# Splitting the first half of a transposed token tile into hi and lo in two steps of 256 columns

## The chip, the cores and the metric

One core of one Trainium2 chip runs the whole program. The metric is the device time of one execution in microseconds (us), as a median over runs. The engines are TensorE (PE), VectorE (DVE), ScalarE (ACT), GpSimd (POOL) and SyncE (SP, which issues the DMAs).

## The reference

The input is 256 tokens of width 1024. The computation, cut to its outline:

```python
x = x + 0.5 * swiglu(rms_norm(x), ...)                  # ffn1, hidden width 2816
x = x + token_mixer(rms_norm(x), ...)                   # three attentions, gated, then w_out
x = x + 0.5 * swiglu(rms_norm(x), ...)                  # ffn2
x = layer_norm(x); memn = layer_norm(mem)               # 256 memory rows
for l in range(2):
    h = x @ w_in[l]
    mix = concat(mla_mixer(h...), nsa_mixer(h...)) @ w_out[l]
    x = layer_norm(ALPHA * x + mix)
    x = layer_norm(ALPHA * x + memory_cross_attn(x, memn, ...))
    x = layer_norm(ALPHA * x + conv_ffn(x, ...))        # w_up, causal conv of 3, gate, w_down
```

All of it is in float32.

## The kernel before

**Products in two parts.** TensorE's operands are fp32r tiles. To keep float32 accuracy every operand is held as two such tiles, a rounded part (hi) and the remainder (lo), and `product` (L299) issues three passes over the contraction chunks: hi·hi for all chunks, then one lo times hi, then the other. `split` (L306) makes the two parts: ACT copies the source to hi (L307), and DVE subtracts hi from the source (L308).

**Token tiles.** The 256 tokens are two tiles of 128, t = 0 and t = 1. Before a matmul that contracts over the width, a tile of 128 tokens by 1024 columns has to be turned. `to_xT` (L357) does that in two halves, j = 0 and 1. `transpose` (L350) turns four blocks of 128x128 on PE into one PSUM tile `tp` of 128x512 (L354, two such buffers), and `split` writes columns j·4 to j·4+3 of `xTh` and `xTl`. So column c of `xTh` (128x128) is what matmul c of the first pass contracts, and columns 0 to 3 come from the first half, 4 to 7 from the second. There are 26 calls of `to_xT`: 24 on the stream itself, two on the memory tiles (there the tiles' names are `mTh` and `mTl`).

**Hand-overs.** `hand_over` (L367) stands between two stages: it turns tile 0, issues a unit of other work if there is one (`fill`: matmuls on the memory), and leaves tile 1 for the middle of the next stage's first unit (`later`, `flush`). `units` (L376) runs the next stage's matmuls, a column group of weights at a time, tile 0 and then tile 1. Weights come by DMA in pieces of 1 MB into two raw buffers `wraw`, and are split in steps of 512 columns into `whi` and `wlo` (`piece`, L282, by the same `split`).

**Order.** Each engine runs its instructions in a fixed order that the framework's scheduler makes from the program. An engine waits at an instruction until what it needs is done, and everything behind it on that engine waits too. So a place where PE needs `xTh` is a chain: four transposes, the copy on ACT, the first matmuls; and DVE's subtraction is needed only by the third pass.

Other names below: `xn` is the normalised tile of an rms norm (Square with its sum on ACT at L329, the product on DVE at L333), `X` the residual stream, `om` the output of nsa_mla, `lat` the latent of mla (its product on DVE, L970, which frees its PSUM tile), `late` the branch that the mixer adds last.

Of the kernel before, what the change touches and what calls it, by code (L numbers as in the profile page):

```python
# [190 lines left out]
class Kern:  # L191
# [165 lines left out]
    def to_xT(self, t, src, dst=None):  # L357

        hi, lo = self.half(dst or self.xT, t)
        for j in range(2):  # L360
            p = self.transpose(src[:, j * 512:j * 512 + 512], 4)
            self.split(hi[:, j * 4:j * 4 + 4], lo[:, j * 4:j * 4 + 4], p)

    def half(self, xT, t):
        return [z[:, :, t * P:t * P + P] for z in xT]
# [1048 lines left out]
```

## Time and profile before

| | |
|---|---|
| median of 3 runs | 1581.88 us (1580.79 to 1583.82) |
| the profiled execution's own time | 1585.94 us |
| its span | 1584.2 us |
| busy: PE, DVE, ACT, POOL | 97%, 68%, 50%, 9% |
| granted TensorE clock, mean | 0.993 |
| chain that ended last, by engine | PE 78%, DVE 9%, issue 5%, DMA 3%, ACT 3%, POOL 2% |

The span is what the profiler recorded of one execution; 1.74 us of that execution's time lie around it. The row of the chain follows the work back from the last instruction and says on which engine the time went. Busy shares are averages over stages.

### The profile page before, as it was taken

Reading aid. Unit: us, or ns where it says so; the run is one execution under the profiler, and the core shown is the slowest. Engines: PE = TensorE matmul, PEld = TensorE weight load, DVE = VectorE, ACT = ScalarE, POOL = GpSimd, SP = SyncE. Lnnn points to the kernel's source line nnn. Section 1 sums busy time; section 2 is a strip of 40 time slices with the busy share of each in tenths; the row PEclk is TensorE's granted clock in tenths of the full one; section 3 lists DMA queues with packets and bytes.
Section 4 is the critical chain, followed back from the end, with each engine's and each line's share of the span. In section 5 each row is a group of like instructions: output and inputs, shape, how many; then the busy total and the mean of one; then the engine's idle time right before and its main releaser. Section 6 shows DMA issues by size and latency. Waiting matters only on the chain.

```text
span 1584.2 us, 23791 instructions
## 1 busy us (share of the span) xinstructions
PE 1541.3 (97%) x8996; PEld 1328.0 (84%) x8996; DVE 1071.3 (68%) x2338; ACT 795.8 (50%) x1752; POOL 150.2 (9%) x158
## 2 busy tenths in 40 slices
PE   8999998999999999999999999999999999999997
PEld 6888876788778788889978988999898879889896
DVE  6756568565698755674676667776774666877675
ACT  5545445355545544444554436655454634456552
POOL 0000001010010000010010002312100010022211
PEclk9999999999999999999999999999999999999999
DMA  7664543444436655543544635554452426355550
GB/s 254 245 221 174 193 142 106 177 150 161 156 127 225 253 203 182 182 155 114 165 150 167 219 124 182 210 211 160 162 208 97 147 75 231 136 200 200 205 194 27
DMA packets 45573, 272.80 MB, mean 172 GB/s; under 512 B 5321, under 2 KB 9201, under 8 KB 16530
## 3 DMA queue, kind: packets, MB, share of 16 engines
q1 hardware_dynamic: 45458, 271.28, 48.1%
q8 instruction: 71, 1.16, 0.3%
q14 instruction: 44, 0.36, 0.1%
HBM read 265.98 MB, written 5.27 MB: 171 GB/s over the span
## 4 chain that ended last, share of the span: by engine, by line
PE 78%; DVE 9%; issue 5%; DMA 3%; ACT 3%; POOL 2%; SPq 0%; DVEq 0%; POOLq 0%; ACTq 0%
PE mm L304 54%; PE acc L304 12%; PE tp L354 3%; DVE wlo L308 3%; PE tp L1051 2%; PE acc L1095 1%; POOL ua L1263 1%; PE tp L1235 1%; PE tp L1129 1%; ACT whi L307 1%; POOL pr L322 1%; DMA wraw<-w_dn 1%; PE acc L1058 1%; PE acc L1220 1%; DMA wraw<-w_up 0%
## 5 line engine op out<-in xcount | busy, mean ns | idle before, releaser
L308 DVE TENSOR_TENSOR wlo<-wraw,whi 128x512 fp32r<-128x512 f32 (+2 forms) x928 | 601.8, 696 | 236.0 <-ACT whi L307 229.3
L307 ACT ACTIVATE whi<-wraw 128x512 fp32r<-128x512 f32 (+2 forms) x928 | 515.5, 619 | 313.3 <-PE mm L304 128.4
L304 PE MATMUL mm<-whi,xTh 128*128 128x512 f32 (+3 forms) x896 | 253.2, 401 | 5.8 <-ACT xTh L307 4.2
L304 PE MATMUL mm<-wlo,xTh 128*128 128x512 f32 (+3 forms) x896 | 240.2, 389 | 0.0
L304 PE MATMUL mm<-whi,xTl 128*128 128x512 f32 (+3 forms) x896 | 239.1, 388 | 0.0
L304 PEld LDWEIGHTS mm<-whi,xTh 128*128 128x128 f32 x896 | 162.8, 190 | 41.9 <-ACT xTh L307 8.2
L304 PEld LDWEIGHTS mm<-wlo,xTh 128*128 128x128 f32 x896 | 167.9, 189 | 35.5 <-issue 1.4
L304 PEld LDWEIGHTS mm<-whi,xTl 128*128 128x128 f32 x896 | 167.7, 188 | 34.1
L322 POOL TENSOR_TENSOR pr<-pv,mhalf 128x1 f32<-128x1 f32 (+3 forms) x44 | 45.7, 1038 | 902.8 <-DVE pv L320 898.1
L304 PE MATMUL mm<-xTh,whi 128*128 128x256 f32 x896 | 127.1, 284 | 3.2 <-DVE ua L1257 1.9
L304 PE MATMUL mm<-xTl,whi 128*128 128x256 f32 x896 | 125.9, 283 | 0.0
L304 PE MATMUL mm<-xTh,wlo 128*128 128x256 f32 x896 | 125.8, 283 | 0.0
L304 PEld LDWEIGHTS mm<-xTh,whi 128*128 128x128 f32 x896 | 116.6, 191 | 5.9 <-ACT th L1261 1.8
L304 PEld LDWEIGHTS mm<-xTl,whi 128*128 128x128 f32 x896 | 115.6, 192 | 0.0
L304 PEld LDWEIGHTS mm<-xTh,wlo 128*128 128x128 f32 x896 | 115.6, 192 | 0.0
L304 PE MATMUL acc<-whi,hh 128*128 128x512 f32 x352 | 112.4, 399 | 2.9 <-ACT hh L1265 2.9
L304 PE MATMUL acc<-wlo,hh 128*128 128x512 f32 x352 | 110.8, 394 | 0.2 <-DVE wlo L308 0.2
L304 PE MATMUL acc<-whi,hl 128*128 128x512 f32 x352 | 109.7, 392 | 0.0
L304 PEld LDWEIGHTS acc<-wlo,hh 128*128 128x128 f32 x352 | 66.6, 189 | 15.1 <-DVE wlo L308 0.7
L304 PEld LDWEIGHTS acc<-whi,hl 128*128 128x128 f32 x352 | 66.5, 189 | 14.3
L304 PEld LDWEIGHTS acc<-whi,hh 128*128 128x128 f32 x352 | 63.4, 189 | 15.1 <-ACT hh L1265 4.0
L1263 POOL TENSOR_TENSOR ua<-ua,ug 128x256 f32<-128x256 f32 x44 | 48.8, 1110 | 251.6 <-DVE ug L1262 175.6
(282 smaller groups left out, 1713.3 us busy)
## 6 DMA issues: line engine op xcount, KB each, us to landing
wraw<-w_ffn_gu SPq DMA_DIRECT2D x42, 1024.0 KB, 4.8
wraw<-w_up SPq DMA_DIRECT2D x40, 1024.0 KB, 4.8
wraw<-w_ffn_dn SPq DMA_DIRECT2D x22, 1024.0 KB, 4.7
wraw<-w_dn SPq DMA_DIRECT2D x22, 1024.0 KB, 4.8
wraw<-w_in_gate SPq DMA_DIRECT2D x12, 1024.0 KB, 4.9
gain<-vec SPq DMA_DIRECT2D x18, 512.0 KB, 4.2
wraw<-w_xk SPq DMA_DIRECT2D x8, 1024.0 KB, 4.7
wraw<-w_fea SPq DMA_DIRECT2D x8, 1024.0 KB, 4.7
```

Source lines behind the costliest of these rows:

```text
L304: self.nc.tensor.matmul(out, L[x], R[y], start=first and i == j == 0, stop=last and i == 2 and j == n - 1)
L307: self.nc.scalar.activation(hi, src, AF.Copy)
L308: self.nc.vector.tensor_tensor(lo, src, hi, op=ALU.subtract)
L322: self.nc.gpsimd.tensor_tensor(r, v, self.mhalf[:, :n], op=ALU.pow)
L354: self.nc.tensor.transpose(p[:, c], src[:, c * P:(c + 1) * P], self.ident)
L1051: nc.tensor.matmul(o[:, h], pt[:, h * (n // P) + k], v(k, h), start=k == 0, stop=k == n // P - 1)
L1058: nc.tensor.matmul(ps[:, h], qT[g][:, h0 + h, t * P:t * P + P], kT[g][:, h0 + h, :n], start=True, stop=True)
L1095: nc.tensor.matmul(pss[i][:, h], nqT[sl, r0 + h, t * P:t * P + P], skT[b][sl, :n], start=True, stop=True)
L1129: nc.tensor.matmul(ps[:30], kc2[:, s, :, :, i], w1[:, i * P:i * P + P], start=i == 0, stop=i == 15)
L1220: nc.tensor.matmul(ps[:, h], qT[:, k, t * P:t * P + P], kT[:, k], start=c == 0, stop=c == 1)
L1235: nc.tensor.matmul(o[:, 2 * h + c], v[:, k, ((h0 + h) * 2 + c) * P:((h0 + h) * 2 + c) * P + P], pt[:, 2 * h + k], start=k == 0, stop=k == 1)
L1263: nc.gpsimd.tensor_tensor(ua, ua, ug, op=ALU.mult)
```

## The change

```diff
     def to_xT(self, t, src, dst=None):
         hi, lo = self.half(dst or self.xT, t)
         for j in range(2):
             p = self.transpose(src[:, j * 512:j * 512 + 512], 4)
-            self.split(hi[:, j * 4:j * 4 + 4], lo[:, j * 4:j * 4 + 4], p)
+            for a, b in (((0, 2), (2, 4)), ((0, 4),))[j]:
+                self.split(hi[:, j * 4 + a:j * 4 + b], lo[:, j * 4 + a:j * 4 + b], p[:, a:b])
```

In each of the 26 calls the first half (j = 0) is split with two copies and two subtractions of 128x256, columns 0 and 1 and then columns 2 and 3, where there were one copy and one subtraction of 128x512. The second half and all other splits stay as they are. The transposes are the same. Line numbers behind L362 go up by one. Because the scheduler orders each engine's instructions anew, more than these rows move.

ACT at the two hand-overs into ffn2 (tile 0, then tile 1). `xTh` are the copies of the split, `xn,ss` the Square of tile 1's norm, `whi` the weights' copies, `th` the gate's first step. Before:

```order
L307 ACTIVATE xTh<-tp 128x4x128 [waits PE_49]
L329 ACTIVATE xn,ss<-X_74 128x1024 [waits DVE_49]
L307 ACTIVATE xTh<-tp 128x4x128 [waits PE_49]
L307 ACTIVATE whi<-wraw 128x512 [waits DMAHW6_49,Activation_49]
L307 ACTIVATE whi<-wraw 128x512 x3
L445 ACTIVATE th<-mm 128x256 [waits PE_49,Pool_49]
L307 ACTIVATE xTh<-tp 128x4x128 [waits PE_49] x2
L307 ACTIVATE whi<-wraw 128x512 [waits DMAHW0_49]
L307 ACTIVATE whi<-wraw 128x512 x3
```


The same place with the change:

```order
L307 ACTIVATE xTh<-tp 128x2x128 [waits PE_49]
L307 ACTIVATE xTh<-tp 128x4x128 [waits PE_49]
L329 ACTIVATE xn,ss<-X_74 128x1024 [waits DVE_49]
L307 ACTIVATE xTh<-tp 128x2x128 [waits DVE_49]
L307 ACTIVATE whi<-wraw 128x512 [waits DMAHW6_49,Activation_49]
L307 ACTIVATE whi<-wraw 128x512 x3
L446 ACTIVATE th<-mm 128x256 [waits PE_49,Pool_49]
L307 ACTIVATE whi<-wraw 128x512 [waits DMAHW0_49]
L307 ACTIVATE xTh<-tp 128x2x128 [waits PE_49]
L307 ACTIVATE xTh<-tp 128x4x128 [waits PE_49]
L307 ACTIVATE whi<-wraw 128x512
L307 ACTIVATE xTh<-tp 128x2x128 [waits DVE_49]
```


In tile 0 the second copy of 128x256 stands behind the second half's copy and behind the Square, and it waits for DVE. In tile 1 the first weight copy, which waits for a DMA, now stands ahead of the three copies of the tile, and another one between them.

PE at the two hand-overs into the second layer's conv_ffn (from the transposes of tile 0, `X_73`, on; `X_74` is tile 1). Before:

```order
L354 MATMUL tp<-c_ident,X_73 128x128 [waits DVE_49]
L354 MATMUL tp<-c_ident,X_73 128x128 x3
L354 MATMUL tp<-c_ident,X_73 128x128 [waits DVE_49,PE_49]
L354 MATMUL tp<-c_ident,X_73 128x128 x3
L304 MATMUL mm<-whi,xTh 128x512 [waits Activation_49]
L304 MATMUL mm<-whi,xTh 128x512 x3
L304 MATMUL mm<-wlo,xTh 128x512 x4
L304 MATMUL mm<-whi,xTl 128x512 [waits DVE_49]
L304 MATMUL mm<-whi,xTl 128x512 x3
```


With the change:

```order
L354 MATMUL tp<-c_ident,X_73 128x128 [waits DVE_49]
L354 MATMUL tp<-c_ident,X_73 128x128 x3
L354 MATMUL tp<-c_ident,X_73 128x128 [waits DVE_49,PE_49]
L354 MATMUL tp<-c_ident,X_73 128x128 x3
L304 MATMUL mm<-whi,xTh 128x512 [waits Activation_49]
L304 MATMUL mm<-whi,xTh 128x512
L304 MATMUL mm<-whi,xTh 128x512 [waits Activation_49]
L304 MATMUL mm<-whi,xTh 128x512
L304 MATMUL mm<-wlo,xTh 128x512 x4
L304 MATMUL mm<-whi,xTl 128x512 [waits DVE_49]
L304 MATMUL mm<-whi,xTl 128x512
L354 MATMUL tp<-c_ident,X_74 128x128 [waits DVE_49,PE_49]
```


The first pass over tile 0 is cut in two: its third matmul has a wait of its own. The transposes of tile 1, which wait for DVE's norm of `X_74`, have come forward into the third pass of tile 0's first unit.

ACT at the same place, from the copy of the last weights ahead of it on. Before:

```order
L307 ACTIVATE whi<-wraw 128x512 [waits DMAHW7_49,DVE_49,PE_49]
L307 ACTIVATE xTh<-tp 128x4x128 [waits PE_49]
L307 ACTIVATE xTh<-tp 128x4x128 [waits DVE_49,PE_49]
L307 ACTIVATE whi<-wraw 128x512 x3
L1280 ACTIVATE ux<-mm 128x512 [waits DMAHW5_49,PE_49]
L307 ACTIVATE xTh<-tp 128x4x128 [waits PE_49]
L307 ACTIVATE xTh<-tp 128x4x128 [waits DVE_49,PE_49]
```


With the change:

```order
L307 ACTIVATE whi<-wraw 128x512 [waits DMAHW7_49,DVE_49,PE_49]
L307 ACTIVATE xTh<-tp 128x2x128 [waits PE_49]
L307 ACTIVATE whi<-wraw 128x512
L307 ACTIVATE xTh<-tp 128x4x128 [waits DVE_49,PE_49]
L307 ACTIVATE whi<-wraw 128x512 x2
L307 ACTIVATE xTh<-tp 128x2x128 [waits DVE_49]
L307 ACTIVATE xTh<-tp 128x2x128 [waits PE_49]
L307 ACTIVATE xTh<-tp 128x2x128 [waits DVE_49]
```


Between the two copies of 128x256 of tile 0 there are now the second half's copy and three weight copies, and the second of them waits for DVE.

## Rows read from the trace of the kernel before

**Rows 1.** The page: busy time of each engine, its share of the span, instructions.
```profile
PE 1541.3 (97%) x8996; PEld 1328.0 (84%) x8996; DVE 1071.3 (68%) x2338; ACT 795.8 (50%) x1752; POOL 150.2 (9%) x158
```

**Rows 2.** Waits of PE: line, releaser: us in total, times, longest.
```profile
PE mm L304 <- ACT xTh L307: 4.8, 14, 0.7
...
PE acc L304 <- ACT hh L1265: 2.9, 3, 1.6
```

**Rows 3.** Groups by form: count, busy, mean ns of one, idle before and releaser.
```profile
L307 ACT ACTIVATE xTh<-tp 128x512 fp32r<-128x512 f32 x58 | 32.5, 594 | 47.5 <-PE tp L354 34.7 <-PE tp L1235 12.7
...
L307 ACT ACTIVATE hh<-tp 128x256 fp32r<-128x256 f32 x44 | 16.7, 379 | 3.9 <-PE tp L354 3.8
...
L308 DVE TENSOR_TENSOR xTl<-tp,xTh 128x512 fp32r<-128x512 f32 x58 | 38.2, 679 | 14.5 <-ACT xTh L307 14.5
...
L308 DVE TENSOR_TENSOR hl<-tp,hh 128x256 fp32r<-128x256 f32 x44 | 18.5, 419 | 4.9 <-ACT hh L307 4.8
```

**Rows 4.** Timeline, om of layer 0, tile 0: start, duration, engine, work, count.
```profile
842.87 1.26 ACT L307 ACTIVATE xTh<-tp 128x512 fp32r<-128x512 f32 x2 [3.08 <-PE tp L354]
...
843.52 1.19 PE L304 MATMUL mm<-whi,xTh 128*128 128x512 f32 x4
...
844.55 1.08 PE L304 MATMUL mm<-wlo,xTh 128*128 128x512 f32 x4
```

**Rows 5.** Timeline, mixer, tile 0 (ACT and PE).
```profile
200.72 0.60 ACT L307 ACTIVATE xTh<-tp 128x512 fp32r<-128x512 f32 x1 [4.00 <-PE tp L354]
...
201.21 1.05 ACT L329 ACTIVATE xn<-X 128x1024 f32<-128x1024 f32 x1
...
201.37 1.20 PE L304 MATMUL mm<-whi,xTh 128*128 128x512 f32 x4 [0.25 <-ACT xTh L307]
```

**Rows 6.** Timeline, ffn2, tile 0 (ACT and PE).
```profile
487.85 0.60 ACT L307 ACTIVATE xTh<-tp 128x512 fp32r<-128x512 f32 x1 [0.92 <-PE tp L354]
...
488.56 1.06 ACT L329 ACTIVATE xn<-X 128x1024 f32<-128x1024 f32 x1
...
488.50 1.19 PE L304 MATMUL mm<-whi,xTh 128*128 128x512 f32 x4 [0.25 <-ACT xTh L307]
```

**Rows 7.** Timeline, ffn2, tile 1 (ACT and PE).
```profile
494.71 1.09 ACT L307 ACTIVATE xTh<-tp 128x512 fp32r<-128x512 f32 x2
...
496.73 2.19 ACT L307 ACTIVATE whi<-wraw 128x512 fp32r<-128x512 f32 x4 [0.93 <-DMA wraw<-w_ffn_dn]
...
495.36 1.19 PE L304 MATMUL mm<-whi,xTh 128*128 128x512 f32 x4 [0.25 <-ACT xTh L307]
```

**Rows 8.** Timeline, conv_ffn of layer 1, tile 0, then tile 1's norm.
```profile
1381.41 1.07 ACT L307 ACTIVATE xTh<-tp 128x512 fp32r<-128x512 f32 x2
...
1382.05 1.20 PE L304 MATMUL mm<-whi,xTh 128*128 128x512 f32 x4 [0.33 <-ACT xTh L307]
...
1382.85 0.67 DVE L308 TENSOR_TENSOR xTl<-tp,xTh 128x512 fp32r<-128x512 f32 x1
...
1385.49 1.41 DVE L347 SCALAR_TENSOR_TENSOR X<-X,pr,gain 128x512 f32<-128x512 f32 x2
```

**Rows 9.** Timeline, om of layer 1, tile 1 (PE and DVE).
```profile
1294.82 1.19 PE L304 MATMUL mm<-whi,xTh 128*128 128x512 f32 x4 [0.25 <-ACT xTh L307]
...
1295.07 1.27 DVE L308 TENSOR_TENSOR xTl<-tp,xTh 128x512 fp32r<-128x512 f32 x2
```

**Rows 10.** Timeline, nsa_mla of layer 0, tile 1 (PE and DVE).
```profile
692.42 1.21 PE L304 MATMUL mm<-whi,xTh 128*128 128x512 f32 x4 [0.45 <-ACT xTh L307]
...
692.80 0.62 DVE L970 TENSOR_SCALAR lat<-mm,pr 128x384 f32<-128x384 f32 x1 [0.73 <-POOL pr L322]
```

**Rows 11.** Timeline, memory_attend of layer 0, tile 1 (PE and DVE).
```profile
874.73 1.33 PE L304 MATMUL mm<-xTh,whi 128*128 128x256 f32 x9 [0.30 <-ACT xTh L307]
...
874.81 1.28 DVE L308 TENSOR_TENSOR xTl<-tp,xTh 128x512 fp32r<-128x512 f32 x2
```

**Rows 12.** Timeline, late branch of the mixer, tile 1 (PE).
```profile
470.76 1.20 PE L304 MATMUL mm<-whi,xTh 128*128 128x512 f32 x4 [0.68 <-ACT xTh L307]
```


## The prediction, made before the changed kernel ran

> **What bounds the kernel now.** First the page's busy times: PE works 97% of the span, DVE 68%, ACT 50% [rows 1]. So a change is worth what it adds to PE's idle time or takes from it, and DVE and ACT matter only where PE waits for them. Next the list of PE's waits: the copies that the change touches (`xTh`, L307) end 14 waits of 0.7 us at most and 4.8 us in all [rows 2], 0.34 us each on average. That is the most that a faster copy could give, and it already says that a large gain isn't there. Then the durations by form, and for each hand-over the timeline of PE, ACT and DVE, laid beside the new order of the three engines.
>
> **What is removed and added.** Nothing leaves; each call gets one instruction more on ACT and one on DVE. The trace has the whole copy, 594 ns, and the whole subtraction, 679 ns, and no 128x256 form of either. The nearest rows are the copy and the subtraction of `hh`, PSUM to SBUF, 128x256: 379 and 419 ns [rows 3]. I take them as they are. So a call costs 2 x 379 - 594 = 164 ns more on ACT and 2 x 419 - 679 = 159 ns more on DVE; times 26 that is 4.3 and 4.1 us on engines with 50% and 32% idle. Spread out it is hidden under PE's matmuls; it costs only inside the hand-overs, which follow.
>
> **The chain at a hand-over.** The first copy still waits for all four transposes (in the order it waits for PE once, behind the fourth), so it starts no sooner. It ends 594 - 379 = 215 ns sooner, and PE's first two matmuls with it. The third matmul needs the second copy. In every hand-over of the new order that copy waits for DVE, and what it waits for is the subtraction of the first piece. So in place of one copy of 594 ns stands copy, subtraction, copy: 379 + 419 + 379 = 1177 ns, with two or three hand-offs between engines of some 0.04 us (the copy ends at 200.72 + 0.60 = 201.32, PE starts at 201.37 [rows 5]) about 1.26 us behind the start. In the kernel before, the third matmul starts 0.52 us behind the first: four of the first pass take 844.55 - 843.52 = 1.03 us [rows 4]; in the mixer that is 201.37 + 0.52 - 200.72 = 1.17 us behind the copy's start. With DVE free and nothing else in ACT's way the third matmul would thus be late by only 0.1 us. Below, "late" is the third matmul's new start less its old one; the passes behind it move with it.
>
> Why the second copy should wait for a subtraction that reads other columns: in the trace the subtraction follows its copy and the two are in a chain through `xTh`, so no row shows whether ACT and DVE could read one `tp` tile together. The Trainium skill, page "PSUM — Partial Sum Buffer", section "PSUM bank collisions raise a hardware error", says that two engines may not access one PSUM bank in the same partitions at once, reads against reads included, and that the compiler adds a dependency between them. By that rule splitting a tile that fills one bank can't let the subtraction of one half run beside the copy of the other; the order agrees (the wait is there), and no run here shows the collision itself. If the bank were no obstacle, the second copy would start when ACT is free; by my sum below that would take some 1.1 us of the 6.2 away (0.35 us at each place where DVE, not ACT, is what holds it), since at the other places ACT's own order holds the copy.
>
> **Place by place** (26 calls; PE's lost time, estimates from the rows).
> - *om, tile 0, both layers.* On ACT stand first copy, second half's copy, second copy. The pair took 1.26 us from 842.87 [rows 4], to 844.13; another 0.38 makes 844.5, so the third matmul starts at 844.5, where it stood at 843.52 + 0.52 = 844.04. Late 0.4 each (some overlap of neighbouring copies taken off): 0.8.
> - *Mixer, tile 0.* The Square (1.05 us from 201.21 [rows 5]) now stands between the two copies. It starts 0.21 earlier, ends at 202.05, the second copy at 202.43, the third matmul 202.48 for 201.89: 0.6.
> - *ffn2, tile 0.* Here both the second half's copy and the Square (1.06 us [rows 6]) stand between: 487.85 + 0.38 + 0.59 + 1.06 + 0.38 = 490.26, for a third matmul at 488.50 + 0.52 = 489.02. Less 0.1 to 0.2 for overlap: 1.1.
> - *ffn2, tile 1.* A weight copy that waits for its DMA (data at 496.73 [rows 7]) now stands ahead of the tile's copies, which began at 494.71. If the data comes at the same time, the first copy starts half a microsecond behind it, near 497.2, and the first matmul at 497.65 for 495.36: 2.3, of which 1.1 is the delay that tile 0 has made already. So 1.2 is new. The DMA's issue waits for a subtraction on DVE that itself stands behind the split now, so it may be later still. Against it: ffn2 runs on at the pace of its weights, and PE stops there anyway for what DVE or a DMA brings; I take 0.7, with 0 and 2.4 as ends.
> - *conv_ffn of layer 1, tile 0.* Four copies stand between the two pieces. Two took 1.07 us from 1381.41 [rows 8], so 0.48 to 0.54 each: 1381.41 + 0.27 + 4 x 0.48 + 0.38 = 1383.98, for 1382.05 + 0.52 = 1382.57. Late 1.4. DVE isn't what holds it: its subtraction began at 1382.85 and now ends 0.42 later. *Tile 1* there: its transposes now come after eight more matmuls of tile 0 (1383.98 + 8 x 0.23 = about 1385.9), and wait for a normalised half that was ready at 1385.49 + 0.7 = 1386.2 and moves back a little. PE loses about 0.3 more than the wait it had. Together 1.7.
> - *om of layer 1, tile 1.* DVE is held until 1295.07 [rows 9], so 1295.07 + 0.42 + 0.38 + 0.08 = 1295.95 for 1294.82 + 0.52 = 1295.34: 0.6.
> - *nsa_mla, tile 1, both layers.* Between second and third matmul the order now has matmuls of the next unit, into a PSUM tile that `lat` frees at 692.80 + 0.62 = 693.42 [rows 10]. The first two matmuls start at 692.42 - 0.21 and end by 692.8, so PE stands 0.7, less the 0.21 won, and a restart (0.1): 0.55 each, 1.1.
> - *memory_attend, tile 1, both layers.* Two short matmuls stand between. DVE is held until 874.81 [rows 11]: second copy done at 874.81 + 0.42 + 0.38 + 0.08 = 875.69; the first four now end by 874.73 - 0.21 + 4 x 0.13 = 875.04. So 0.65 less 0.21, 0.45 each: 0.9.
> - *Gains.* In the late branch, tile 1, the first copy now comes ahead of a weight copy, and the wait of 0.68 [rows 12] goes almost wholly: -0.6. At the mixer's and the first om's tile 1, other matmuls hide the second copy: -0.2 each. At the start the orders differ much: -0.3, within half a microsecond either way.
> - *Nothing* at the nine other calls, where units on the memory or whole passes of other matmuls lie between the copies and their readers. Without that cover each would cost 0.4 as in om.
>
> Sum: 0.8 + 0.6 + 1.1 + 0.7 + 1.7 + 0.6 + 1.1 + 0.9 - 1.3 = 6.2 us. On the profiled execution's own 1585.94 us (span 1584.2) that is 1592.1. That execution lies 4.06 us above the median of 1581.88; the same difference on the median gives **1588.1 us**. About 0.2% (3.2 us) is what a measurement of this kernel can tell from no change.
>
> **Rivals.**
> - *The split does what it says.* At all 14 waits PE starts 0.215 us sooner and the third matmul is on time: -3.0, 1578.9 us. For it: the difference of 594 and 379 ns is sure, and the plain chain makes the third matmul only 0.1 late, less than what is won if other matmuls stand between. It decides if the second copy ends within 0.57 us of the first's end; with DVE's 0.42 and its own 0.38 it can't, so only where there is cover. Chance 0.12.
> - *The delays are given back.* PE stops later in the same stage for something that isn't delayed, and the lost time is taken from that stop. For it: `hh` alone ends three waits of 2.9 us, one of 1.6 [rows 2], in the conv_ffn and ffn stages, which the two dearest places (ffn2 and layer 1's conv_ffn, 3.5 together) feed. If these 3.5 go, 2.7 stay: 1584.6, no change that can be told. Against it: what ACT and DVE make there is delayed by the same amount, since PE feeds them. Chance 0.23.
> - *ffn2's DMA decides.* Issue and landing move by the whole delay of DVE: 2.4 for 0.7, and the new order of the following weights adds as much again: 1588.1 + 3.4 = 1591.5. Chance 0.15.
> - My forecast, 1585.5 to 1590.5: 0.50.
>
> Outside the counted places the scheduler has reordered weight splits in ffn1 and both conv_ffn stages; PE's waits there are few, and I price them at nothing, within 2 us either way. Range: 1579.5 to 1593.5. It leaves out most of the first rival's lower half, and the third's upper end with these 2 us. Chances: the first rival's 1578.9 lies just at the bound, so half of its 0.12 is faster and half no change; of the second, 0.18 is no change, 0.03 faster and 0.02 slower; my forecast and the third are slower but for 0.01. Together: faster 0.09, within 0.2% 0.25, slower 0.66.
>
> **What would show it.** Right: copies of 128x256 near 380 ns, 52 on the 26 calls (48 to `xTh`, four to `mTh`); PE's waits for `xTh` grown from 4.8 to about 9 us, most of them at the third matmul; the Square between the copies in the mixer; a copy of the tile in ffn2 that begins after the weight's DMA landed. Wrong: third matmuls that don't wait; the lost time of ffn2 gone by the time memory starts; a copy of 256 columns well above 400 ns, by which every place would cost more.

## The result, and the profile after

The changed kernel took 1599.54 us (median of 6 runs, 1594.66 to 1604.27), beside 1582.85 us of the kernel before (6 runs): a ratio of 1.010 with a 95% interval of 1.0077 to 1.0122, some 16 us slower. Timed again with the later experiments it was 1.0085 (1.0068 to 1.0102). The profiled execution took 1596.49 us, with a span of 1594.7 us: 10.5 us more than the one of before. The runs of one kernel, before and after, differ by several us, so a median says more than one trace; the trace says where.

The page of the kernel after, part 1, answers to [rows 1]; below it are lines of its list of PE's waits, which answer to [rows 2] (us in total, times, longest).

```profile
PE 1545.0 (97%) x8996; PEld 1328.4 (83%) x8996; DVE 1073.6 (67%) x2364; ACT 798.4 (50%) x1778; POOL 150.8 (9%) x158
```

```profile
PE mm L304 <- ACT xTh L307: 10.8, 12, 2.8
...
PE acc L304 <- ACT hh L1266: 3.0, 3, 1.6
...
PE mm L304 <- DVE lat L971: 1.0, 2, 0.5
```

PE's waits for the copies went from 4.8 to 10.8 us, and the longest from 0.7 to 2.8. ACT and DVE are as idle as before. The groups by form (count, busy, mean ns, idle before) answer to [rows 3]:

```profile
L307 ACT ACTIVATE xTh<-tp 128x512 fp32r<-128x512 f32 x34 | 20.1, 595 | 15.5 <-PE tp L1236 13.4 <-PE tp L354 1.5
L308 DVE TENSOR_TENSOR xTl<-tp,xTh 128x256 fp32r<-128x256 f32 x48 | 20.0, 417 | 12.9 <-ACT xTh L307 12.7
L307 ACT ACTIVATE xTh<-tp 128x256 fp32r<-128x256 f32 x48 | 18.2, 378 | 45.9 <-PE tp L354 42.6 <-DVE xTl L308 3.1
```

The durations of the new instructions were right: 378 and 417 ns, for 379 and 419 taken from the `hh` rows. Both traces have the same 8996 matmuls, so the start of one and the same group of transposes in the two timelines tells by how much PE is late there:

| transposes (start of the group) | before | after | late by |
|---|---|---|---|
| mixer, tile 0 | 200.08 | 202.00 | 1.9 |
| ffn2, tile 0 | 487.21 | 487.98 | 0.8 |
| ffn2, tile 1 | 494.08 | 496.42 | 2.3 |
| memory, in ffn2 | 529.47 | 535.92 | 6.4 |
| om, layer 0, tile 0 | 842.23 | 849.13 | 6.9 |
| om, layer 0, tile 1 | 849.11 | 856.49 | 7.4 |
| conv_ffn, layer 0, tile 0 | 935.89 | 943.59 | 7.7 |
| nsa_mla, layer 1, tile 1 | 1147.58 | 1153.86 | 6.3 |
| om, layer 1, tile 0 | 1286.65 | 1294.98 | 8.3 |
| conv_ffn, layer 1, tile 0 | 1380.68 | 1390.51 | 9.8 |
| the last matmul | 1574.92 | 1585.49 | 10.6 |

The lag also falls in places, because the trace of before lost time of its own there: the granted clock has a mean of 0.66 at 212 to 217 us and of 0.57 at 970 to 974 us, where the trace after has 1.00 in the same matmuls, and two stops of PE near 1494 and 1502 us have no counterpart after.

More than half is lost in ffn2, between 488 and 506 us. Its timeline after (start, us, engine, work; at the end in brackets the idle time before and what ended it) answers to [rows 6, 7]:

```profile
488.61 1.03 ACT L307 ACTIVATE xTh<-tp 128x256 fp32r<-128x256 f32 x2 [0.92 <-PE tp L354]
489.82 1.06 ACT L329 ACTIVATE xn<-X 128x1024 f32<-128x1024 f32 x1 [0.18 <-DVE X L890]
490.79 0.19 ACT L329 ACTIVATION_READ_ACCUMULATOR xn<-X 128x1 f32 x1
490.88 0.36 ACT L307 ACTIVATE xTh<-tp 128x256 fp32r<-128x256 f32 x1
...
489.70 1.01 DVE L308 TENSOR_TENSOR xTl<-tp,xTh 128x256 fp32r<-128x256 f32 x2
490.63 0.68 DVE L308 TENSOR_TENSOR wlo<-wraw,whi 128x512 fp32r<-128x512 f32 x1
...
499.28 0.63 ACT L307 ACTIVATE whi<-wraw 128x512 fp32r<-128x512 f32 x1 [2.21 <-DMA wraw<-w_ffn_dn]
499.82 0.85 ACT L307 ACTIVATE xTh<-tp 128x256 fp32r<-128x256 f32 x2
...
491.30 0.73 PE L304 MATMUL mm<-whi,xTh 128*128 128x512 f32 x2 [1.51 <-ACT xTh L307]
...
496.42 1.03 PE L354 MATMUL tp<-c_ident,xn 128*128 128x128 f32 x8
500.23 3.40 PE L304 MATMUL mm<-whi,xTh 128*128 128x512 f32 x8 [2.78 <-ACT xTh L307]
503.43 1.40 PE L304 MATMUL mm<-wlo,xTh 128*128 128x512 f32 x4
...
491.39 0.33 SPq L291 DMA_DIRECT2D wraw<-w_ffn_dn  x1
```

In the trace of before, the same subtraction of a weight piece and the same DMA's issue:

```profile
488.44 0.69 DVE L308 TENSOR_TENSOR wlo<-wraw,whi 128x512 fp32r<-128x512 f32 x1
...
489.15 0.39 SPq L291 DMA_DIRECT2D wraw<-w_ffn_dn  x1
```

Tile 0: the second copy runs at 490.88, behind the Square, and PE stops 1.51 us at its third matmul. Tile 1: its transposes end at 497.45, but ACT is waiting for the data of `w_ffn_dn`, whose DMA was issued at 491.39 and in the trace of before at 489.15. The issue follows the end of a subtraction (`wlo`) that frees the raw buffer, at 491.31 for 489.13; on DVE that subtraction now stands behind two of the tile's. The copies of the tile, with nothing else to wait for, start at 499.82; PE stops for 2.78 us. And then the next eight matmuls, all hi·hi, take 3.40 us, where four took 1.07 elsewhere. The windows after (length, busy time and count for each engine, granted TensorE clock, DMA share, GB/s) show why:

```profile
core 0: us, PE busy (x) PEld busy (x) DVE busy (x) ACT busy (x) POOL busy (x), PEclk, DMA share, GB/s
...
497.00:500.00 3.00, 0.46 (x5) 0.22 (x2) 0.95 (x4) 0.79 (x3) 0.00 (x0) 1.00 0.85 269
500.00:503.00 3.00, 2.77 (x7) 2.14 (x8) 2.62 (x6) 2.50 (x6) 0.99 (x1) 0.62 0.78 291
503.00:506.00 3.00, 3.00 (x12) 2.49 (x11) 3.00 (x6) 0.17 (x1) 0.00 (x0) 0.81 0.05 22
506.00:510.00 4.00, 4.00 (x20) 3.26 (x19) 2.45 (x6) 2.68 (x6) 0.00 (x0) 1.00 0.45 147
```

Before the stop the granted clock is 1.00, the level of 2.4 GHz; behind it the clock is for a while at 1.2 GHz (0.62 and 0.81 are means of a stretch with both levels). The stop itself cost 2.5 us (2.78 less the 0.25 of before [rows 7]) and the matmuls behind it some 1.6 more: twelve of them take 4.60 us (500.23 to 504.83), where in the trace of before twelve take 3.02 from 495.36 on.

Two more places, the same timeline view after. At nsa_mla of layer 1, tile 1, other weight copies stand ahead of the second copy, and they too wait for a DMA:

```profile
1157.65 1.15 ACT L307 ACTIVATE whi<-wraw 128x512 fp32r<-128x512 f32 x2 [2.00 <-DMA wraw<-w_tok]
1158.70 0.36 ACT L307 ACTIVATE xTh<-tp 128x256 fp32r<-128x256 f32 x1
...
1156.41 1.07 PE L304 MATMUL mm<-whi,xTh 128*128 128x440 f32 x4 [0.46 <-DVE lat L971]
1157.32 0.56 PE L304 MATMUL mm<-wlo,xTh 128*128 128x440 f32 x2
1159.12 0.74 PE L304 MATMUL mm<-whi,xTh 128*128 128x512 f32 x2 [1.24 <-ACT xTh L307]
```

PE stops twice, 0.46 for `lat` as foreseen and 1.24 for the second copy, which was not. At conv_ffn of layer 1 it is as foreseen, the second copy behind three weight copies, at 1393.55 for an estimate of 1383.6 and a lag of 9.8:

```profile
1392.51 1.14 ACT L307 ACTIVATE whi<-wraw 128x512 fp32r<-128x512 f32 x2
1393.55 0.38 ACT L307 ACTIVATE xTh<-tp 128x256 fp32r<-128x256 f32 x1
...
1393.98 0.73 PE L304 MATMUL mm<-whi,xTh 128*128 128x512 f32 x2 [1.58 <-ACT xTh L307]
1394.55 1.51 PE L304 MATMUL mm<-wlo,xTh 128*128 128x512 f32 x4
1395.86 1.05 PE L304 MATMUL mm<-whi,xTl 128*128 128x512 f32 x2
1396.71 1.05 PE L354 MATMUL tp<-c_ident,X 128*128 128x128 f32 x4
1398.24 0.57 PE L304 MATMUL mm<-whi,xTh 128*128 128x512 f32 x1 [0.47 <-ACT xTh L307]
```

### The profile page after: what moved, and what is told of

It is laid out like the page before. It is cut to its first block, busy times and chain, and to the rows that moved or that the text cites. A ratio compares the mean times of both kernels' runs of the same rounds, so it can differ in the third digit from the quotient of the medians.

```text
span 1594.7 us, 23845 instructions
## 1 busy us (share of the span) xinstructions
PE 1545.0 (97%) x8996; PEld 1328.4 (83%) x8996; DVE 1073.6 (67%) x2364; ACT 798.4 (50%) x1778; POOL 150.8 (9%) x158
## 4 chain that ended last, share of the span: by engine, by line
PE 72%; DVE 11%; DMA 6%; issue 6%; ACT 3%; POOL 2%; SPq 0%; DVEq 0%; POOLq 0%; ACTq 0%
PE mm L304 49%; PE acc L304 10%; DVE wlo L308 4%; PE tp L354 3%; PE tp L1052 2%; DMA wraw<-w_up 2%; ACT whi L307 1%; PE acc L1096 1%; POOL ua L1264 1%; PE tp L1236 1%; PE tp L1130 1%; DMA wraw<-w_xo 1%; DMA wraw<-w_ffn_gu 1%; POOL pr L322 1%; DMA wraw<-w_tok 1%
## 5 line engine op out<-in xcount | busy, mean ns | idle before, releaser
L304 PE MATMUL mm<-whi,xTh 128*128 128x512 f32 (+3 forms) x896 | 256.6, 404 | 14.0 <-ACT xTh L307 10.3
L322 POOL TENSOR_TENSOR pr<-pv,mhalf 128x1 f32<-128x1 f32 (+3 forms) x44 | 48.9, 1112 | 908.3 <-DVE pv L320 904.7
L304 PEld LDWEIGHTS acc<-whi,hh 128*128 128x128 f32 x352 | 63.3, 188 | 15.8 <-ACT hh L1266 4.1
```

The costliest lines, as they stand in the source:

```text
L304: self.nc.tensor.matmul(out, L[x], R[y], start=first and i == j == 0, stop=last and i == 2 and j == n - 1)
L322: self.nc.gpsimd.tensor_tensor(r, v, self.mhalf[:, :n], op=ALU.pow)
```

## The experiments

All ratios are to the kernel before, measured next to it on the same chip, with 95% intervals.

**1. Both copies ahead of both subtractions.**

```diff
-            for a, b in (((0, 2), (2, 4)), ((0, 4),))[j]:
-                self.split(hi[:, j * 4 + a:j * 4 + b], lo[:, j * 4 + a:j * 4 + b], p[:, a:b])
+            for a, b in (((0, 2), (2, 4)), ((0, 4),))[j]:
+                self.nc.scalar.activation(hi[:, j * 4 + a:j * 4 + b], p[:, a:b], AF.Copy)
+            for a, b in (((0, 2), (2, 4)), ((0, 4),))[j]:
+                self.nc.vector.tensor_tensor(lo[:, j * 4 + a:j * 4 + b], p[:, a:b], hi[:, j * 4 + a:j * 4 + b], op=ALU.subtract)
```

> As the change, but both copies of the first half stand ahead of both subtractions in the code, so no copy waits for a subtraction; ACT's order then has the two copies side by side at all 26 calls. Theory A (the loss comes from the second copy's wait for DVE's subtraction and from what the scheduler puts ahead of it): the loss of 10.6 us of span vanishes, and the first matmul of each exposed hand-over starts 0.2 us sooner, so 2 to 4 us under the kernel before; no wait of PE for xTh over 0.7 us. Rival B (two small instructions for one, 8.4 us of ACT and DVE work, cost the time by themselves): still 8 to 17 us above the kernel before. Rival C (any new order of the schedule costs as much): 5 us or more above it, with new waits at other places.

Measured: 0.9992 (0.998 to 1.0004), median 1582.65 for 1584.62 us; the profiled span is 1580.1 us. In its list of PE's waits the copies have nearly vanished:

```profile
PE mm L304 <- ACT xTh L363: 0.7, 3, 0.3
```

It has every instruction of the change, in the same sizes, and none of its loss. That refutes rival B (the instructions' own cost) and C (any new order). The gain of the trace is some 4 us, that of the medians 2, which the interval can't tell from none. Place by place its trace shows what the shorter first copy is worth: the same matmul, by count, comes 0.2 us sooner behind each exposed hand-over (nsa_mla, om and memory_attend, in both layers).

**2. Two PSUM tiles for the two pieces.**

```diff
-        for j in range(2):
-            p = self.transpose(src[:, j * 512:j * 512 + 512], 4)
-            ...
+        for a, b in ((0, 2), (2, 4), (4, 8)):
+            p = self.transpose(src[:, a * P:b * P], b - a)
+            self.split(hi[:, a:b], lo[:, a:b], p)
```

> As the change, but the two pieces of the first half are transposed into two PSUM tiles of their own (three tiles a call, two buffers), so the first copy waits for two transposes and not four, and the second copy for no subtraction; the subtractions stay between the copies in the code. Theory A: no loss, and up to 0.4 us sooner at an exposed hand-over, 3 to 6 us under the kernel before, less what the third tile costs by waiting for a free buffer (the second half's copy goes back behind the weight copies at several places): between -5 and +2 us. Rival B: 8 to 17 us above the kernel before. Rival C: 5 us or more above.

Measured: 1.0039 (1.0025 to 1.0052), median 1590.18 for 1584.62, 5.6 us more; outside what theory A gave. Its second copy waits for no subtraction, yet PE waits for the copies 17 times, and the transposes of the third tile twice for a subtraction that has to free their buffer:

```profile
PE mm L304 <- ACT xTh L307: 9.0, 17, 1.7
...
PE tp L354 <- DVE xTl L308: 1.1, 2, 0.9
```

So it leaves a third of the loss and doesn't tell what the shared bank alone costs: other waits took the place of the one removed. The longest, 1.69 us before a matmul at 1388.2 in layer 1's conv_ffn, is once more copies that stand behind a weight copy, which waited 1.61 us for the DMA of `w_up`; the others are not taken apart.

**3. The change at the two calls into ffn2 alone** (`self.calls` counts the calls of `to_xT`).

```diff
+            cut = j == 0 and self.calls in (6, 7)
+            for a, b in ((0, 2), (2, 4)) if cut else ((0, 4),):
+                self.split(...)
```

> The change at the two hand-overs into ffn2 alone, the other 24 calls as before. Theory A, with the trace of the change: tile 0 loses 1.6 us, and tile 1 some 4.1, since a weight copy that waits for its DMA stands ahead of the tile's copies on ACT as in the change; so 4.5 to 6 us of span above the kernel before, all of it between 487 and 503 us. Rival D (PE's clock or the whole machine is slower with the change, the places do not add up): under 1 us. Rival B: 2/26 of the loss, under 1.3 us.

Measured: 1.0034 (1.0017 to 1.0051), median 1588.66 for 1584.62. The two calls alone cost 4 to 5 us, nearly what theory A says and more than rivals B and D allow. In the execution that was profiled the data had come in time: ACT took the weight copy at 497.06 without a wait for the DMA, PE's stops in ffn2 were 1.01, 0.45 and 0.55 us, the granted clock stayed at 1.00, and the span was 1583.3 us, no more than before. So in that execution the place cost nothing, and with data in time there was no long stop. That the other executions' cost hangs on when the DMA lands is likely, but one trace doesn't show it; the 12 runs spread from 1583.17 to 1598.02 us, the two longest at a mean granted clock of 0.985 where the shortest had 0.994. The mean of the twelve clocks is 0.991, that of the 32 runs of before beside them 0.9935.

**4. Subtraction in two steps, copy whole.**

```diff
+            self.nc.scalar.activation(hi[:, j * 4:j * 4 + 4], p, AF.Copy)
+            for a, b in (((0, 2), (2, 4)), ((0, 4),))[j]:
+                self.nc.vector.tensor_tensor(..., op=ALU.subtract)
```

> The copy of the first half stays whole, only its subtraction is made in two steps of 256 columns: DVE's half of the change alone. Theory A: nothing that can be told, -1 to +1.5 us, since the third pass that reads the result comes 1.8 us behind the first. Rival B: about half the loss, 5 to 8 us. Rival C: 5 us or more either way.

Measured: 0.9986 (0.9974 to 0.9997), median 1583.03 for 1584.62 us, a little below what theory A gave. DVE's half of the change costs nothing.

**5 to 7. The change again, without both calls into ffn2, and without tile 1's.** The condition of experiment 3 is always true, `self.calls not in (6, 7)`, and `self.calls != 7`.

> The change itself once more, beside the next three. 9 to 17 us above the kernel before. Theory F (part of the loss is TensorE's clock, which falls after the long stop at ffn2's tile 1): the executions lie in two groups, those with a mean granted clock of 0.992 or more 9 to 12 us above the kernel before, those at 0.990 or less 17 to 21 us above. Rival (the clock is the chip's affair, not the kernel's): the clocks of the four kernels of this call are spread alike.

> The change at all calls but the two into ffn2; there no weight copy stands ahead of tile 1's copies any more. Theory A, with the steps read from the trace of the change: 10.6 less the 5.7 of ffn2, so 4 to 6 us of span above the kernel before. Theory F: no execution under a granted clock of 0.990, so the median is 4 to 7 us above too. Rival C (any new order costs as much): 9 us or more.

> The change at all calls but the one for tile 1 into ffn2, whose first half is copied whole; the new order still has the weight copy, which waits for a DMA, ahead of that whole copy. Theory G (what costs there is the weight copy ahead on ACT, not the piece chain): the wait of 1.5 to 3 us before tile 1's first matmul in ffn2 stays, 8 to 16 us above the kernel before as with the change. Rival H (the chain of copy, subtraction and copy in tile 1 costs it): the stop shrinks to under 0.7 us, and the span to 5 to 7 us above the kernel before.

Measured: 1.0085 (1.0068 to 1.0102), 1.0049 (1.0034 to 1.0064) and 1.0101 (1.0074 to 1.0128). Without ffn2's two calls 7.7 us remain of 14 to 17; undoing tile 1's alone saves nothing. The two groups that theory F gave for experiment 5 did not show: its four runs were 1594.77 to 1599.46 at clocks of 0.989 to 0.992, not in order. What F says of experiment 6's clocks did: its four runs all had 0.993 and lay within 1.3 us, while those of experiment 7 had 0.987 to 0.993; but 7.7 us is more than the 4 to 7 that A and F gave. Experiment 7's 16 us by the ratio, 17 by the medians, lie at the upper end of theory G.

The clocks of all runs together speak against F's rival. The four sets of runs in which tile 0 of ffn2 is split as the change does it (the change twice, experiments 3 and 7) have mean clocks of 0.990 to 0.991; every other kernel here, the one of before and experiments 6 and 12 too, has 0.993 to 0.995. So the change's split of that tile brings the clock down, in some executions more than in others.

The timeline of experiment 7 in ffn2 (here lines are one higher):

```profile
500.57 0.38 ACT L449 ACTIVATE th<-mm 128x256 f32<-128x256 f32 x1 [4.99 <-PE mm L305]
501.50 0.63 ACT L308 ACTIVATE whi<-wraw 128x512 fp32r<-128x512 f32 x1 [0.54 <-DMA wraw<-w_ffn_dn]
502.03 1.07 ACT L308 ACTIVATE xTh<-tp 128x512 fp32r<-128x512 f32 x2
...
493.56 0.73 PE L305 MATMUL mm<-whi,xTh 128*128 128x512 f32 x2 [1.51 <-ACT xTh L308]
494.13 1.75 PE L305 MATMUL mm<-wlo,xTh 128*128 128x512 f32 x4
495.68 1.91 PE L305 MATMUL mm<-whi,xTl 128*128 128x512 f32 x4
...
502.67 1.19 PE L305 MATMUL mm<-whi,xTh 128*128 128x512 f32 x4 [1.32 <-ACT xTh L308]
```

The tile's copy is whole (128x512), and it stands behind the weight copy all the same, and PE stops 1.32 us. In this execution the clock fell already behind tile 0's stop of 1.51: the eight matmuls from 494.13 on end at 497.59, 3.46 us for 2.00 in the trace after (491.86 to 493.86), where the same stop left the clock at 1.00.

**8. Copies in two steps, subtraction whole.**

```diff
+            for a, b in (((0, 2), (2, 4)), ((0, 4),))[j]:
+                self.nc.scalar.activation(hi[:, j * 4 + a:j * 4 + b], p[:, a:b], AF.Copy)
+            self.nc.vector.tensor_tensor(lo[:, j * 4:j * 4 + 4], p, hi[:, j * 4:j * 4 + 4], op=ALU.subtract)
```

> The copy of the first half is made in two steps, the subtraction stays whole behind both: ACT's half of the change alone. Theory A: like the kernel with both copies first, -4 to 0 us, since no copy waits for a subtraction and the copies stand side by side. Rival B (more instructions cost): half of the loss, 4 to 8 us above.

Measured: 0.9985 (0.997 to 0.9999), median 1580.60 for 1582.62 us, as theory A gave.

**9 to 11. The second half split in place of the first; copies of 128 and 384 columns; experiment 8 again.** In 9 the pairs are `(((0, 4),), ((0, 2), (2, 4)))[j]`, in 10 `(((0, 1), (1, 4)), ((0, 4),))[j]` in the code of experiment 8.

> The change mirrored: the first half's split stays whole, the second half (columns 4 to 7) is split in two steps. As many added instructions, the same chain of copy, subtraction and copy, and in ffn2 again a weight copy that waits for its DMA between the two copies of tile 1; but its columns 6 and 7 are needed only by the second group of twelve matmuls, some 3 us behind the first matmul. Theory A: the loss is mostly gone, -2 to +3 us. Rival B (the added instructions cost) or rival C (any new order costs): 8 us or more above.

> Copies only, but in steps of 128 and 384 columns (one matmul's operand, then three), both ahead of the whole subtraction. Theory A: the first copy is another 0.1 us shorter, and the second, 0.49 us by the slope of the copies, ends when the second matmul wants it; -4 to -1 us against the kernel before, within 2 us of the steps of 256. Rival: the third instruction's fixed cost eats it, 0 to +2 us.

> The copies in two steps of 256 with a whole subtraction behind both, once more, beside the other two: -4 to 0 us against the kernel before, as in the first look (0.9985).

Measured: 1.001 (0.9995 to 1.0024), 0.9992 (0.9978 to 1.0007) and 0.9981 (0.9967 to 0.9995). The mirrored change has the same chain, and the same weight copies between its copies, and costs nothing that can be told: its columns are wanted late enough. That finer steps bring more isn't shown. Experiment 8's version has the two lowest ratios of the twelve, the second time 1579.87 for 1584.37 us, but the intervals overlap those of experiments 1, 4 and 10, so it can't be told from them; and experiment 4, which leaves the copy whole, lies as low as its first.

**12. The change without tile 0's call into ffn2** (`self.calls != 6`).

> The counterpart of the kernel that undid tile 1: the change at all calls but the one for tile 0 into ffn2. Tile 1 keeps the chain of copy, subtraction and copy, but in this order the weight copy that waits for its DMA stands behind its three copies again. Theory G (what costs in ffn2 is that weight copy ahead on ACT, with the stop of tile 0): tile 1's first matmul waits 0.5 us at most, and the time is that of the kernel with both ffn2 calls undone, 6 to 9 us above the kernel before. Rival H (tile 1's chain costs it): 11 us or more above.

Measured: 1.0043 (1.0023 to 1.0064), 1591.98 for 1583.87 us: the same as with both calls undone. In ffn2:

```profile
498.16 1.03 ACT L308 ACTIVATE xTh<-tp 128x256 fp32r<-128x256 f32 x2
499.56 0.38 ACT L308 ACTIVATE xTh<-tp 128x256 fp32r<-128x256 f32 x1 [0.36 <-DVE xTl L309]
501.87 2.20 ACT L308 ACTIVATE whi<-wraw 128x512 fp32r<-128x512 f32 x4 [1.92 <-DMA wraw<-w_ffn_dn]
...
500.00 0.73 PE L305 MATMUL mm<-whi,xTh 128*128 128x512 f32 x2 [0.67 <-ACT xTh L308]
```

The chain of tile 1 is here, bare: the second copy waits for DVE (0.36), PE 0.67 us. The weight's data comes as late as ever, 501.87, and nobody on the path waits for it. So of ffn2's loss the chain in tile 1 is half a microsecond, and the rest is tile 0's stop with the order that its split brings: rival H falls, theory G stands.

## Why the prediction was wrong

The direction and the cause were right, the size was not: 1588.1 forecast, range to 1593.5, 1599.54 measured. By its steps:

- **Durations, chain, and what the second copy waits for**: right, 378 and 417 ns. With the copies first the whole loss goes (experiment 1), and DVE's half alone costs nothing (4).
- **Places with the bare chain**: about right. The lag in the table grows by 0.5 at om, layer 0, tile 0 (0.4 forecast), and by 1.5 at ffn2, tile 0 (1.1). Taken at the same matmul by count it grows by 0.6 at nsa_mla of layer 0 (0.55), 0.5 and 0.2 at memory_attend (0.45 each) and 1.15 at om of layer 1 (1.0), and it shrinks by 0.6 in the late branch (0.6).
- **ffn2, tile 1: the step that failed.** The text saw the weight copy ahead of the tile's copies and the later issue of its DMA, and took "0.7, with 0 and 2.4 as ends", because ffn2 would make up for it. Measured: 6.4 - 2.3 = 4.1 us in the trace, and nothing made up: the lag is still 6.9 at om. The issue moved by 2.2 us and the data came 2.6 us later (499.28 for 496.73 [rows 7]); the stop, 2.5 us longer than the one of before, was just above the upper end of the range, and the clock behind it, of which the text had nothing, added some 1.6. The two ffn2 calls cost 4 to 5 us alone (experiment 3) and 6 to 9 in the company of the others (13.5 to 15.8 by the two ratios of the change, less 6.8 to 7.8 by those of experiments 12 and 6), for 1.8 forecast.
- **nsa_mla, layer 1, tile 1**: 0.55 forecast for the stop at `lat`; the trace has that stop, and 1.24 more for the second copy behind two weight copies that wait for `w_tok`. The same omission: the order showed these copies, and their DMA was not looked up.
- **The start**: -0.3 forecast; the lag is 1.9 at the mixer. Its size differs from execution to execution: the same transposes, at 200.08 before, start at 202.00 after, at 201.66, 200.40 and 202.47 in experiments 5, 6 and 12, which have nearly the same order there, and at 200.85 in experiment 1. The matmuls show what makes most of it. In the trace after, those of 128x512 follow each other at 0.43 us until 19.2 us, the pace that they have at 501 to 503 us at the lower clock; in the trace of before they do so at 0.23 us from 15.1 on. (The clock column of the windows shows none of this so early.) In experiments 7, 12, 5, 3 and 6 the slow pace lasts until about 19.9, 19.2, 18.4, 16.9 and 15.5 us, and the lag at one matmul behind it is 3.4, 2.8, 2.3, 1.4 and 1.1 us, in the trace after 2.6. Why TensorE gets to its faster pace later stays open.
- **conv_ffn, layer 1**: 1.7 forecast. PE stops 1.58 and 0.47 us, 1.4 more than the two stops of before, so that term was about right; but the clock falls behind the first stop (a mean of 0.50 from 1395.0 to 1398.4), and the six matmuls from 1394.55 on take 2.36 us. At the same matmul by count the lag grows from 9.8 to 13.0 across the two tiles, and to 13.8 behind the waits for `hh`. It ends at 10.6, because PE of before stops 0.24, 0.67 and 1.66 us at 1482, 1494 and 1502 (for `ua`, a weight copy, and `ua`), and PE after does not. That looks like the second rival's mechanism, but experiments 3 and 9, only 2.3 us late and 1.8 early there, lack these stops too; so it isn't shown that the delay was given back. The last of these stops, before:

```profile
1502.03 1.19 PE L304 MATMUL mm<-xTh,whi 128*128 128x256 f32 x8 [1.66 <-DVE ua L1257]
```

In conv_ffn of layer 0 the trace of before has a stretch at half the clock, 971 to 973.5, which the trace after and most of the experiments' don't have (those of experiments 3, 10 and 11 have one there). It took 2 us of the lag away by chance.

```profile
971.00:973.50 2.50, 2.50 (x7) 1.92 (x7) 2.50 (x5) 2.11 (x5) 0.82 (x2) 0.50 0.34 62
```

- **The rivals**: the first (the split does what it says) fell with its own condition, that the second copy is on time. Where the condition is met, in experiments 8 and 11, the ratios stand 2.4 and 3.0 us below the kernel before, for the 3.0 that it promised; but experiments 1 and 10, which meet it too, show 1.3, and experiment 4, which splits no copy, 2.2, so the gain isn't shown. The second read the `hh` waits as lying in ffn stages too; all three are in the two conv_ffn stages (967.6, 970.3 and 1409.0). The third (ffn2's DMA decides) was the right mechanism, too small by half, and had a chance of 0.15.
- **The clock, which the sum put at nothing.** The medians of the first comparison lie 16.7 us apart, the profiled executions 10.6. Both profiled executions have a mean granted clock of 0.993: what the change lost to it behind its stops, the one of before lost elsewhere. The six runs of the change have 0.990 in the mean, from 0.993 at 1595 us down to 0.986 at 1604, and the sets of runs of before beside the experiments 0.993 to 0.994. A mean clock that is lower by 0.0035 for 1600 us is worth some 5.6 us, an estimate that takes PE as busy throughout, and with the 10.6 it gives 16. That lower clock goes with the change's split of ffn2's tile 0 (experiments 3 and 7 have both, 6 and 12 neither).
- What stays open: why the clock falls in some executions and not in others at the same place, and how the lost time by the medians divides between stops and clock.

## What to carry to other kernels

Splitting a copy to start its reader sooner can help only if the pieces stay next to each other on their engine: put all copies ahead of the work that reads the same PSUM tile. Even then the gain here was 0.2 us at each exposed place, too little to tell in the time of the whole. In the code of one split after the other, each piece waits for the other engine, and a scheduler fills that gap with whatever it thinks is ready, on an engine that then works strictly in that order. So after such an edit look at every instruction that now stands between the pieces or ahead of them, and for each that waits for a DMA look up in the trace when that DMA lands; price that, not the chain.

## What the runs showed that I had not expected

Short stops of TensorE can cost more than their length. Behind the stop of 2.78 us the granted clock was at 1.2 GHz for a while (means of 0.62 and 0.81 at 500 to 506 us after the change), which added some 1.6 us; in experiment 7 the same happened behind a stop of 1.51 (eight matmuls in 3.46 us for 2.00). But a stop doesn't decide it by its length alone. In the 14 traces, from 300 us on, each of the four stops of 2.1 to 3 us had such a fall in it or less than 2 us behind its end, 7 of the 34 stops of 1.2 to 1.8 us had one, and none of the 38 of 0.9 to 1.2 us; the stop of 1.51 us in the trace after had none. And the clock fell without a stop as well: in experiment 4's trace its mean is 0.51 from 1255.6 to 1262.6 us, where PE had been busy throughout the 3.6 us before, with small matmuls.
